# A decoder layer on one core: where four buffers, queues and small calculations are placed

## The chip, the core and the metric

The kernel runs on one core of a Trainium2 chip. The metric is the device time of one execution in microseconds (us). The kernel before was timed three times: 1932.65, 1937.01 and 1935.72 us, median 1935.72 us. A profile of a further execution shows what every engine did: PE (TensorE matmuls), PEld (its weight loads), DVE (VectorE), ACT (ScalarE), POOL (GpSimd) and SP (SyncE, which here only issues DMAs). An engine works through its own list of instructions in order; a DMA issued from SP, ACT or POOL stands in that engine's list as well.

## The reference

One layer over S = 2048 tokens of D = 1024 channels, all in float32. Names are those of the weights.

```python
hn = rms_norm(h, mix_pre_g)
proj = hn @ w_in                            # q, k, v and the GLU input
attn_out = sliding_window_attention(q, k, v, attn_sinks, rel_bias)   # window 128
conv_out = conformer_conv(u, ...)           # GLU, causal conv of 31 taps, LayerNorm, swish, w_conv_pw
mixed = concatenate([attn_out, conv_out]) @ w_out
h = h + rms_norm(mixed, mix_post_g)
hn = rms_norm(h, ffn_pre_g)
ff = (silu(hn @ w_gate) * (hn @ w_up)) @ w_down
h = h + rms_norm(ff, ffn_post_g)
```

## The kernel before, in words

**Precision.** A float32 product is made of three matmuls: each operand is split into a high part (an ACT copy, L888, L782 or L133) and a low part (a DVE subtraction, written through L85), and high x high, high x low and low x high are added up in a PSUM bank. A step of twelve matmuls so needs one ACT copy and one DVE subtraction for its weight tile w@F. There are four PSUM banks named mm, three named tr and one named ct; a bank that PE wants again has to be read out by ACT or DVE first.

**Stages.** Tokens go in four tiles of 512 (w = 0 to 3). A is the input projection, B the attention, C the convolution: its taps are 480 DVE instructions (fc@C<-glu@C), whose results are written to y_scr (L618), loaded again (L630) and turned by PE through the ct bank (L602). W is the output projection of a tile with its norm and residual (`stage_w`, `norm_w`). F is the gate and up projection and G the down projection, both as seven products of half-size blocks (Strassen and Winograd) for two tiles together: first for tiles 0 and 1, then for 2 and 3. `stage_pre` does the first two products of some blocks ahead of time and stores one result of each in the DRAM tensor keeps (from ACT, 36 stores); `stage_p1` does the rest and puts the products of gate and up into the DRAM tensor mids (L1129, L1160, L1166, L1169); `stage_p2` (G) loads these and multiplies with w_down and its block sums.

**Order.** The program is written as one main chain (A, then W of tile 1, F, G, F, G) and lanes beside it (taps, attention, W of tile 0, W of tiles 2 and 3, block sums of w_down) which are advanced by credits as the main chain goes on. A scheduler then sets the final order of the instructions on each engine from these. A buffer name such as fa, chl or gb is a ring with a fixed count of slots: a new user of a slot waits until the last user has been read.

**W of tile 0** runs beside A of tile 2 and 3. `stage_w` loads two rows of mixT at a time (`load`, L804, from SP), ACT and DVE split them (`operand`, L782), PE multiplies (mm@W), ACT copies the first results out of the bank (mid@W, L757). Its first two rows use two slots of the ring fa, which stages A, F and G use as well.

**The norms of W.** `norm_w` needs two reciprocal roots of 128x4 numbers for a tile, each by three Newton steps in `rsqrt`. For w < 3 they are done on POOL (four instructions a step, L159 to L162), for w = 3 on DVE (three a step). ACT then scales the rows by the second one (L873).

**Kept results.** In `stage_p1`, `fetch` (L1097 to L1101) loads the kept result of the next block into a slot of gb, a DMA issued by SP. ACT copies it into a PSUM bank (L1132) before the block's products add to it. There are 19 such loads in F of tiles 0 and 1 and 15 in F of tiles 2 and 3; two further ones are taken from `stage_pre`.

**G's loads.** In `stage_p2` the DRAM rows of mids are loaded one by one (L1237): the first two into the ring at, the others into fa, which still holds the last results of F on their way to mids. The w_down halves go into mb (L1241).

Of the kernel before, what the change touches and what calls it, by code (L numbers as in the profile page):

```python
# [23 lines left out]
D = 1024  # L24
DFF = 2816
P = 128
T = 512
# [10 lines left out]
def layer_kernel(ctx, tc, x, xT, cols, rows, sinks, relb, onehot, w_in, w_four, w_pw, w_out, w_gate, w_up, w_down, out):  # L38
    nc = tc.nc
# [9 lines left out]
    def nm(s):  # L49
        uid[0] += 1  # L50
        return f"{s}@{lab[0]}_{uid[0]}"
# [3 lines left out]
    def t_(tag, shape, dt=F32):  # L55
        return sb.tile(list(shape), dt, tag=tag, name=nm(tag), bufs=BUFS[tag])

    def f4(tag, shape=(P, D)):
        return t_(tag, shape)

    def f2(tag, shape=(P, T)):
        return t_(tag, shape)

    def hl(tag):
        return t_(tag, (P, 2, T), F32R)

    def sm(n, dt=F32):
        kind = "A" if lab[0][0] == "G" else lab[0][0]
        return sb.tile([P, 8], dt, tag="sm" + kind, name=nm("sm"), bufs={"C": 8, "W": 4}.get(kind, 16))[:, 0:n]
# [80 lines left out]
    def rsqrt(ssq, n, mean_over, beside_taps=True):  # L150
        v = sm(n)
        y = sm(n)
        t = sm(n)
        vts(v, ssq, 1.0 / mean_over, EPS, ALU.mult, ALU.add)
        vts(y.bitcast(I32), v.bitcast(I32), 1, None, ALU.logical_shift_right)
        vts(y.bitcast(I32), y.bitcast(I32), -1, 0x5F3759DF, ALU.mult, ALU.add)
        for _ in range(3):
            if beside_taps:
                ptt(t, y, y, ALU.mult)  # L159
                ptt(t, t, v, ALU.mult)  # L160
                nc.gpsimd.tensor_scalar(t, t, -0.5, 1.5, ALU.mult, ALU.add)
                ptt(y, t, y, ALU.mult)  # L162
            else:
                vtt(t, y, y, ALU.mult)
                stt(t, v, -0.5, t, ALU.mult, ALU.mult)
                stt(y, t, 1.5, y, ALU.add, ALU.mult)
        return y
# [453 lines left out]
    def stage_tail(t, sink=None):  # L621
        L = f"C{t}"
        lab[0] = L
        yt = t_("yt", (P, 4, 4 * P))
        ycs = []
        turn = turner(yt, ycs)
        for c in range(4):
            lab[0] = L
            y = f2("fc")
            nc.sync.dma_start(y, y_scr[c, :, t * T : (t + 1) * T])  # L630
            ycs.append(y)
            turn(c)
            yield 0.5
        yield from conv_tail(t, yt, sink)
# [34 lines left out]
    def spare_tile():  # L669
        if not spare:  # L670
            spare.append(t_("mb", (P, 2, T)))
        return spare[0]
# [89 lines left out]
    def load_gb(row):  # L762
        gb = []
        for n in range(2):
            t = f2("gb")
            nc.sync.dma_start(t, rows[row, n * T : (n + 1) * T].partition_broadcast(P))
            gb.append(t)
        return gb

    def post_scale(acc, gb, r):  # L770
        for n in range(2):
            cs = slice(n * T, (n + 1) * T)
            tied(stt(acc[:, cs], acc[:, cs], r, gb[n], ALU.mult, ALU.mult))

    def stage_w(w, spill, G, atag, htag, mtag, bank_of, norm=None):
        L = f"W{w}"
        lab[0] = L
        acc = [f4(atag) for _ in range(4)]

        def operand(m):  # L780
            a = hl(htag)
            act(a[:, 0], m, AF.Copy)  # L782
            vtt(a[:, 1], m, a[:, 0].bitcast(F32), ALU.subtract)
            return [a]

        def acts(gi, ms=None):
            return [operand(m) for m in ms or load(gi)]

        conv = []
        tail = stage_tail(w, lambda v: conv.append(operand(v))) if w > 1 else ()  # L790
        for y in tail:
            if y == YL2:
                break
            yield y
        lab[0] = L

        stage = spare_tile() if w == 1 else None

        def load(gi):
            ms = []  # L800
            pair_ = stage if w == 1 else t_("wx", (P, 2, T)) if w > 1 and gi == 0 else None
            for c in range(G * gi, G * gi + G):
                ms.append(pair_[:, c % 2] if pair_ is not None else f2(mtag))
                nc.sync.dma_start(ms[-1], mixT[c, :, w * T : (w + 1) * T])  # L804
            return ms

        first = load(0)
        gb = load_gb(0) if w > 1 else None
        if w != 1:
            yield 5.0 if w == 0 else 8.0  # L810
            lab[0] = L
        nxt = acts(0, first)
        for gi in range(KC // G):
            if w > 1 and G * gi == 4:
                yield from tail
                lab[0] = L
            aa = nxt if w < 2 or G * gi < 4 else conv[G * gi - 4 : G * gi - 4 + G]
            for n in range(2):
                lab[0] = L
                more = gi + 1 < KC // G and (w < 2 or G * gi + G < 4)  # L820
                if n == 0 and more:
                    if w < 2 and G * gi + G == 4:
                        ld.until(f"C{w}")
                        lab[0] = L
                    rows_next = load(gi + 1)
                if n == 1 and more:
                    nxt = acts(gi + 1, rows_next)
                src = w_out[2 * gi : 2 * gi + 2] if gi < 2 else w_join[2 * gi - 4 : 2 * gi - 2]
                ws = weight(src[:, :, n * T : (n + 1) * T].rearrange("c p t -> p c t"),
                            lo_out[n, 2 * gi : 2 * gi + 2], w > 0, on_pool=False)  # L830
                yield from block_half(acc, list(zip(aa, ws)), n, gi == 0, L, bank_of)
        last = norm_w(w, spill, acc, mtag, gb)
        if norm:
            norm(last)
        else:
            yield from last

    def norm_w(w, spill, acc, mtag, gb):
        L = f"W{w}"
        lab[0] = L  # L840
        gb = gb or load_gb(0)
        ssq = sm(4)
        for s in range(4):
            act(junk, acc[s], AF.Square, accum_out=ssq[:, s : s + 1])
            yield 0.5
            lab[0] = L
        r = rsqrt(ssq, 4, D, w < 3)
        yield 3
        lab[0] = L
        ssq2 = sm(4)  # L850
        for s in range(4):
            lab[0] = L
            post_scale(acc[s], gb, r[:, s : s + 1])
            r0 = w * T + s * P
            if s == (2 if mtag == "fa" else 0):
                xt = f4("wx")
                nc.sync.dma_start(xt, x[r0 : r0 + P])
                vtt(acc[s], xt, acc[s], ALU.add)
            else:
                for n in range(2):  # L860
                    cs = slice(n * T, (n + 1) * T)
                    xt = f2(mtag if s == 1 or w > 1 else "fa")
                    nc.sync.dma_start(xt, x[r0 : r0 + P, cs])
                    vtt(acc[s][:, cs], xt, acc[s][:, cs], ALU.add)
            nc.sync.dma_start(h_scr[r0 : r0 + P], acc[s])
            act(junk, acc[s], AF.Square, accum_out=ssq2[:, s : s + 1])
            yield 5.0
        lab[0] = L
        r2 = rsqrt(ssq2, 4, D, w < 3)
        yield 3  # L870
        lab[0] = L
        for s in range(4):
            act(acc[s], acc[s], AF.Copy, scale=r2[:, s : s + 1])  # L873
            if spill:
                r0 = w * T + s * P
                nc.scalar.dma_start(hn_scr[r0 : r0 + P], acc[s])
        yield 0.1
        hns[w] = acc
# [176 lines left out]
    def stage_p1(ws, ops, mid, keep):  # L1055
# [32 lines left out]
        kept = {}  # L1088
# [8 lines left out]
        def fetch(m):  # L1097
            if m < PRE:
                lab[0] = L
                kept[m] = f2("gb")  # L1100
                nc.sync.dma_start(kept[m], keep[m])  # L1101

        loads(0)
        sums(0)
# [5 lines left out]
        for q, (m, j, i, nst) in enumerate(todo):  # L1110
# [4 lines left out]
            pr = MATS[m][1]  # L1115
# [56 lines left out]
            if j == 1:  # L1172
                fetch(m + 1)
# [44 lines left out]
    def stage_p2(ws, am, td, last=False):  # L1218
# [5 lines left out]
        rawa, rawb, opsd = {}, {}, {}  # L1224
# [7 lines left out]
        def load(i):  # L1232
            if i < len(steps):
                lab[0] = L
                ty, pr = steps[i]
                rawa[i] = f2("fc" if last else "at" if i < 2 else "fa")
                nc.sync.dma_start(rawa[i], am[ty, pr])  # L1237
                if pr % 2 == 0:
                    rb = t_("raw" if last else "mb", (P, 2, T))
                    for j in range(min(2, npr - pr)):  # L1240
                        nc.sync.dma_start(rb[:, j], source(ty, pr + j))  # L1241
                        rawb[i + j] = rb[:, j]
# [16 lines left out]
        kept = {}  # L1259
# [71 lines left out]
        for i in range(nn):  # L1331
            ty, pr = steps[i]
# [20 lines left out]
        for b in range(4):  # L1353
# [3 lines left out]
            ssq = sm(1)  # L1357
# [5 lines left out]
            r = rsqrt_one(ssq, sse[:, b : b + 1])  # L1363
# [248 lines left out]
```

## Time and profile before

| | us |
|---|---|
| median of three runs | 1935.72 |
| the profiled execution | 1937.05 |
| its span, first to last instruction | 1934.7 |
| PE busy in it | 1897.4 |
| DVE busy | 1492.1 |
| ACT busy | 970.4 |
| POOL busy | 211.5 |

The span is 2.35 us shorter than the profiled execution's own time, and the sum of the prediction is made against that own time. PE is busy for 98% of the span, so all that can be gained without leaving work out lies in PE's gaps and in stretches in which its granted clock is below 1. A row of a timeline gives the start, the duration, the engine, the line, what is written and read, how many like instructions follow each other, and in brackets how long the engine stood idle just before and what released it.

### The profile page before, as it was taken

The page shows a single profiled execution, that of the slowest core. Times are in us where ns is not written, and L with a number is a line of the kernel's source. Part 1 is how long each engine was busy: PE and PEld are TensorE (multiplying, and loading weights), DVE is VectorE, ACT ScalarE, POOL GpSimd, SP SyncE. Part 2 cuts the span into 40 slices and gives each one's busy share as a digit, 9 for nine tenths or more (in the row PEclk, how much of TensorE's full clock was granted, in tenths as well). Part 3 has the DMA queues.
Part 4 walks back from the last instruction along what each step waited for, and adds up shares of the span by engine and source line. Part 5 has one row for each costly group of instructions (what it writes and reads, how often), then busy time and mean ns, then how long its engine had stood idle before and what let it go on. Part 6 is the DMA issues. An engine that isn't in the chain of part 4 may idle for free.

```text
span 1934.7 us, 26719 instructions
## 1 busy us (share of the span) xinstructions
PE 1897.4 (98%) x8714; PEld 1535.7 (79%) x8714; DVE 1492.1 (77%) x2760; ACT 970.4 (50%) x1911; POOL 211.5 (11%) x311
## 2 busy tenths in 40 slices
PE   9999998999999999999999999999999999999997
PEld 7777776777778878877878878888888888888886
DVE  6999999887876999988988775788566665455557
ACT  5455444656667433433445574676434333345443
POOL 2010012112010000000000010010033333211000
PEclk9999999999999999999999999999999999999999
DMA  9887756669668775787396687699544443376664
GB/s 332 313 279 234 226 171 213 196 229 342 197 239 283 242 249 200 230 279 266 125 320 224 216 308 233 219 346 314 196 166 151 165 151 109 131 240 193 209 193 156
DMA packets 227707, 439.35 MB, mean 227 GB/s; under 512 B 22728, under 2 KB 48752, under 8 KB 227568
## 3 DMA queue, kind: packets, MB, share of 16 engines
q1 hardware_dynamic: 206256, 403.04, 62.6%
q10 hardware_dynamic: 19392, 28.32, 4.1%
q0 software_dynamic: 1920, 6.29, 0.8%
q8 instruction: 68, 1.11, 0.2%
q14 instruction: 71, 0.58, 0.1%
HBM read 318.54 MB, written 119.02 MB: 226 GB/s over the span
## 4 chain that ended last, share of the span: by engine, by line
PE 67%; DVE 16%; DMA 11%; issue 3%; ACT 1%; POOL 1%; SPq 0%; DVEq 0%; ACTq 0%; POOLq 0%
PE mm@F L108 35%; PE mm@G L108 18%; DVE fc@C L85 7%; PE tr@W L108 4%; PE mm@A L108 4%; PE mm@W L108 3%; PE tr@B L108 1%; DMA glu@C<-glu_scr 1%; DVE w@F L85 1%; DMA mids<-fa@F 1%; DMA chl@F<-w_gate 1%; DVE fa@F L85 1%; DVE p@B L493 1%; DMA wx@G<-w_down 1%; DMA fa@G<-mids 1%
## 5 line engine op out<-in xcount | busy, mean ns | idle before, releaser
L85 DVE SCALAR_TENSOR_TENSOR fc@C<-glu@C,colt,fc@C 128x512 f32<-128x512 f32 x480 | 353.3, 753 | 1.9
L108 PE MATMUL mm@F<-hl@H,w@F 128*128 128x512 f32 x1056 | 254.6, 390 | 0.1
L108 PEld LDWEIGHTS mm@F<-hl@H,w@F 128*128 128x128 f32 x1056 | 197.8, 188 | 42.0 <-ACT gb@F L1143 0.9
L108 PE MATMUL mm@G<-hl@G,hl@G 128*128 128x512 f32 x924 | 226.8, 395 | 3.7 <-ACT hl@G L888 3.0
L108 PEld LDWEIGHTS mm@G<-hl@G,hl@G 128*128 128x128 f32 x924 | 171.5, 189 | 41.6 <-ACT hl@G L888 3.8
L888 ACT ACTIVATE w@F<-chl@F 128x512 fp32r<-128x512 f32 x220 | 135.3, 625 | 130.1 <-PE mm@F L108 124.7
L108 PE MATMUL mm@G<-w@G,hl@G 128*128 128x512 f32 x876 | 199.5, 389 | 0.0
L108 PE MATMUL mm@A<-hl@A,w@A 128*128 128x512 f32 x792 | 192.1, 393 | 1.4 <-DVE w@A L85 1.1
L108 PEld LDWEIGHTS mm@G<-w@G,hl@G 128*128 128x128 f32 x876 | 164.4, 188 | 34.1
L108 PEld LDWEIGHTS mm@A<-hl@A,w@A 128*128 128x128 f32 x792 | 147.0, 188 | 34.6 <-issue 1.7
L85 DVE TENSOR_TENSOR w@F<-chl@F,w@F 128x512 fp32r<-128x512 f32 x198 | 144.2, 732 | 35.3 <-ACT w@F L888 34.9
L108 PE MATMUL mm@F<-mid@H,w@F 128*128 128x512 f32 x528 | 131.3, 392 | 3.5 <-DVE fa@F L85 3.5
L108 PE MATMUL mm@F<-ql@H,w@F 128*128 128x512 f32 x528 | 130.5, 391 | 4.3 <-ACT w@F L888 3.3
L108 PE MATMUL mm@F<-p@H,w@F 128*128 128x512 f32 x528 | 129.0, 389 | 0.0
L108 PE MATMUL mm@F<-x@H,w@F 128*128 128x512 f32 x528 | 128.3, 391 | 0.0
L108 PEld LDWEIGHTS mm@F<-mid@H,w@F 128*128 128x128 f32 x528 | 99.4, 189 | 25.1 <-DVE fa@F L85 4.4
L108 PEld LDWEIGHTS mm@F<-ql@H,w@F 128*128 128x128 f32 x528 | 98.4, 188 | 25.7 <-ACT w@F L888 4.1
L108 PEld LDWEIGHTS mm@F<-x@H,w@F 128*128 128x128 f32 x528 | 98.5, 188 | 21.9 <-ACT w@F L888 0.8
L108 PEld LDWEIGHTS mm@F<-p@H,w@F 128*128 128x128 f32 x528 | 99.0, 188 | 20.7 <-ACT at@F L1146 0.2
L108 PE MATMUL mm@W<-w@W,hl@W 128*128 128x512 f32 x384 | 102.0, 411 | 8.2 <-ACT hl@W L782 5.1
L85 DVE TENSOR_TENSOR w@G<-raw@G,w@G 128x512 fp32r<-128x512 f32 x73 | 51.3, 703 | 67.0 <-ACT w@G L888 66.0
L133 ACT ACTIVATE w@A<-raw@A 128x512 fp32r<-128x512 f32 x104 | 63.0, 624 | 64.6 <-DMA raw@A<-w_in 36.5
(314 smaller groups left out, 3197.7 us busy)
## 6 DMA issues: line engine op xcount, KB each, us to landing
mids<-fa@F SPq DMA_DIRECT2D x154, 256.0 KB, 2.8
raw@A<-w_in SPq DMA_DIRECT2D x52, 512.0 KB, 5.3
w@A<-lo_in SPq DMA_DIRECT2D x84, 256.0 KB, 4.7
fc@G<-mids SPq DMA_DIRECT2D x77, 256.0 KB, 3.5
fa@G<-mids SPq DMA_DIRECT2D x75, 256.0 KB, 4.6
w@W<-lo_out SPq DMA_DIRECT2D x48, 256.0 KB, 3.8
chl@F<-w_gate SPq DMA_DIRECT2D x22, 512.0 KB, 4.0
raw@F<-w_gate SPq DMA_DIRECT2D x22, 512.0 KB, 3.8
```

Of the source, the lines that this page charges most:

```text
L85: r = op(*args, **kw)
L108: r = nc.tensor.matmul(*args, **kw)
L133: act(w[:, 0], raw, AF.Copy)
L493: read = nc.vector.tensor_tensor_reduce(out=pr[:, h], in0=os[g][:, j, P:], in1=bias[0][:, h], op0=ALU.add, op1=ALU.max, scale=1.0, scalar=NEG,
L888: act(w[:, 0], x, AF.Copy)
```

## The change

Four edits, each independent of the others:

```diff
@@ stage_w, load (1) @@
-            pair_ = stage if w == 1 else t_("wx", (P, 2, T)) if w > 1 and gi == 0 else None
+            pair_ = stage if w == 1 else t_("wx", (P, 2, T)) if gi == 0 else None
@@ norm_w (2) @@
-        r = rsqrt(ssq, 4, D, w < 3)
+        r = rsqrt(ssq, 4, D, w == 2)
...
-        r2 = rsqrt(ssq2, 4, D, w < 3)
+        r2 = rsqrt(ssq2, 4, D, w == 2)
@@ stage_p1, fetch (3) @@
-                nc.sync.dma_start(kept[m], keep[m])
+                nc.scalar.dma_start(kept[m], keep[m])
@@ stage_p2, load (4) @@
-                rawa[i] = f2("fc" if last else "at" if i < 2 else "fa")
-                nc.sync.dma_start(rawa[i], am[ty, pr])
+                if not last and i < 8:
+                    if i % 2 == 0:
+                        pair_ = t_("chl", (P, 2, T))
+                        nc.sync.dma_start(pair_, am[ty, pr : pr + 2].rearrange("j p t -> p j t"))
+                        rawa[i], rawa[i + 1] = pair_[:, 0], pair_[:, 1]
+                else:
+                    rawa[i] = f2("fc" if last else "fa")
+                    nc.sync.dma_start(rawa[i], am[ty, pr])
```

(1) The first two rows of W of tile 0 go into the single buffer wx in place of two slots of fa. (2) The roots of tiles 0 and 1 are made on DVE (9 instructions of Newton steps a call) in place of POOL (12 a call); four calls change. (3) The 34 loads of kept results are issued by ACT in place of SP. (4) In the first G the first eight rows of mids come as four loads of two rows each into the ring chl; at is no longer used there, and fa only from the ninth row on.

The scheduler places the instructions anew. Three places show it.

**First place: W of tile 0 beside A.** SP's list before, where the taps' result y_scr, the loads of rows fa@W<-mixT and weights follow each other:

```order
L132 DMA w@A_573_3525<-lo_in 128x512
L143 DMA raw@A_609_3700<-w_in 128x1024
L618 DMA y_scr<-fc@C_420_2645 128x512
L593 DMA glu@C_544_3397<-glu_scr 128x542
L804 DMA fa@W_561_3488<-mixT 128x512
L804 DMA fa@W_562_3490<-mixT 128x512
L383 DMA glu_scr<-fa@A_550_3441 128x512
L804 DMA fa@W_565_3498<-mixT 128x512
L143 DMA raw@W_626_3809<-w_out 128x2x512
L804 DMA fa@W_566_3500<-mixT 128x512
```

And SP's list now (buffer numbers are one lower behind the pair that left the ring):

```order
L132 DMA w@A_572_3524<-lo_in 128x512
L143 DMA raw@A_608_3699<-w_in 128x1024
L804 DMA fa@W_564_3497<-mixT 128x512
L804 DMA fa@W_565_3499<-mixT 128x512
L618 DMA y_scr<-fc@C_420_2645 128x512
L593 DMA glu@C_544_3397<-glu_scr 128x542
L383 DMA glu_scr<-fa@A_550_3441 128x512
```

The loads of the third and fourth row, which stood behind y_scr, stand ahead of it; those of the first two are gone from here and stand some fifty entries earlier, in the wx buffer. On PE the transposes of the taps' result (L602) moved against the projection A. PE's list before:

```order
L602 MATMUL ct@C_593_3637<-ident,fc@C_592_3635 128x128 x4
L108 MATMUL mm@W_656_3959<-w@W_655_3955,hl@W_585_3605 128x512
L535 MATMUL tr@B_672_4051<-ident,p@B_541_3375 128x128 x4
L108 MATMUL mm@A_669_4021<-mid@A_503_3142,w@A_667_4015 128x512 x3
L108 MATMUL mm@A_669_4021<-mid@A_504_3146,w@A_667_4015 128x512 x3
L108 MATMUL mm@A_669_4021<-mid@A_505_3150,w@A_667_4015 128x512 x3
L108 MATMUL mm@A_669_4021<-mid@A_506_3154,w@A_667_4015 128x512 x3
```

PE's list now:

```order
L108 MATMUL mm@A_668_4020<-hl@A_521_3264,w@A_667_4017 128x512 x3
L108 MATMUL mm@A_668_4020<-hl@A_522_3268,w@A_667_4017 128x512 x3
L108 MATMUL mm@A_668_4020<-hl@A_523_3272,w@A_667_4017 128x512 x3
L108 MATMUL mm@A_668_4020<-hl@A_524_3276,w@A_667_4017 128x512 x3
L535 MATMUL tr@B_671_4050<-ident,p@B_541_3375 128x128 x4
L602 MATMUL ct@C_592_3636<-ident,fc@C_591_3634 128x128 x4
```

The 24 matmuls of this block of A, which followed the transposes, now precede them; counted from the program's start, 1772 matmuls stood ahead of them before and 1801 stand there now.

**Second place: the end of W of tile 0 on ACT.** ACT's list before, from the first scaling by the root (L873) to the first copy out of a bank of tile 1 (mid@W, L757):

```order
L873 ACTIVATE x@W_557_3484<-x@W_557_3484,sm@W_777_4666 128x1024
L873 ACTIVATE x@W_558_3485<-x@W_558_3485,sm@W_777_4666 128x1024
L873 ACTIVATE x@W_559_3486<-x@W_559_3486,sm@W_777_4666 128x1024
L782 ACTIVATE hl@W_850_5101<-mb@J_341_2174 128x512
L873 ACTIVATE x@W_560_3487<-x@W_560_3487,sm@W_777_4666 128x1024
L876 DMA hn_scr<-x@W_557_3484 128x1024
L782 ACTIVATE hl@W_851_5104<-mb@J_341_2174 128x512
L876 DMA hn_scr<-x@W_558_3485 128x1024
L445 ACTIVATE ql@A_789_4769<-mm@A_787_4737 128x512
L133 ACTIVATE w@W_838_5030<-raw@W_837_5028 128x512
L133 ACTIVATE w@W_839_5033<-raw@W_837_5028 128x512
L876 DMA hn_scr<-x@W_559_3486 128x1024
```

ACT's list now:

```order
L782 ACTIVATE hl@W_849_5094<-mb@J_341_2174 128x512
L782 ACTIVATE hl@W_850_5097<-mb@J_341_2174 128x512
L445 ACTIVATE ql@A_788_4762<-mm@A_786_4730 128x512
L133 ACTIVATE w@W_837_5023<-raw@W_836_5021 128x512
L133 ACTIVATE w@W_838_5026<-raw@W_836_5021 128x512
L757 ACTIVATE mid@W_789_4775<-mm@W_798_4797 128x512
L873 ACTIVATE x@W_557_3484<-x@W_557_3484,sm@W_776_4662 128x1024
L873 ACTIVATE x@W_558_3485<-x@W_558_3485,sm@W_776_4662 128x1024
L873 ACTIVATE x@W_559_3486<-x@W_559_3486,sm@W_776_4662 128x1024
L873 ACTIVATE x@W_560_3487<-x@W_560_3487,sm@W_776_4662 128x1024
L876 DMA hn_scr<-x@W_557_3484 128x1024
L757 ACTIVATE mid@W_790_4776<-mm@W_813_4887 128x512
```

The splits of tile 1, a copy of A and the first copy out of a bank moved from behind the scalings to ahead of them; the second copy out of a bank still stands behind.

**Third place: kept results in F of tiles 0 and 1.** SP's list before, at the load of the seventeenth (names with 14xx are its block's):

```order
L1193 DMA td<-fc@G_1449_8566 128x512
L1071 DMA chl@F_1471_8744<-w_gate 128x1024
L1193 DMA td<-fc@G_1448_8565 128x512
L1160 DMA mids_4775<-fa@F_1430_8466 128x512
L1101 DMA gb@F_1463_8679<-keeps_4780 128x512
L1166 DMA mids_4775<-fa@F_1430_8466 128x512
```

ACT's list now, at the same load:

```order
L1143 ACTIVATE gb@F_1457_8640<-mm@F_1456_8627 128x512
L1101 DMA gb@F_1462_8666<-keeps_4773 128x512
L888 ACTIVATE w@F_1463_8671<-chl@F_1460_8660 128x512
L1146 ACTIVATE at@F_1459_8658<-mm@F_1455_8625 128x512
L888 ACTIVATE w@F_1465_8691<-chl@F_1460_8660 128x512
L1132 ACTIVATE mm@F_1473_8740<-gb@F_1462_8666 128x512
L888 ACTIVATE w@F_1467_8712<-chl@F_1461_8663 128x512
```

And ACT's list now at the fifteenth load:

```order
L1143 ACTIVATE gb@F_1422_8408<-mm@F_1421_8395 128x512
L888 ACTIVATE w@F_1428_8437<-chl@F_1425_8428 128x512
L1101 DMA gb@F_1427_8434<-keeps_4773 128x512
L1132 ACTIVATE mm@F_1438_8506<-gb@F_1427_8434 128x512
L888 ACTIVATE w@F_1430_8457<-chl@F_1425_8428 128x512
```

The load no longer stands behind stores to td and mids on SP; on ACT it stands ahead of the copy that needs it (L1132), with three instructions between at the seventeenth and none at the fifteenth.

## Prediction

> **What bounds the kernel now.** I read the page first, then the list of what PE waited for, then the timeline around each wait, and last the clock behind it.
>
> ```profile
> PE 1897.4 (98%) x8714; PEld 1535.7 (79%) x8714; DVE 1492.1 (77%) x2760; ACT 970.4 (50%) x1911; POOL 211.5 (11%) x311
> ```
> ```profile
> PE mm@W L108 <- ACT hl@W L782: 5.1, 1, 5.1
> PE mm@F L108 <- DVE fa@F L85: 3.5, 2, 2.7
> ...
> ```
>
> PE is the bound, and the first rows of its waits (total, times, longest) name single waits, not a steady one. A wait costs more than its length if the clock falls. The next rows show the stretches right behind four of them (length, PE busy, PEld, DVE, ACT, POOL, granted clock, DMA share, GB/s).
>
> ```profile
> 327.40:332.40 5.00, 5.00 (x15) 4.06 (x16) 4.26 (x17) 1.22 (x2) 0.43 (x1) 0.67 0.96 279
> 474.70:482.70 8.00, 8.00 (x30) 6.14 (x30) 2.85 (x11) 3.86 (x7) 0.00 (x0) 0.61 0.91 311
> 862.70:867.70 5.00, 5.00 (x15) 3.95 (x16) 5.00 (x9) 2.30 (x4) 0.00 (x0) 0.66 0.79 255
> 999.00:1004.00 5.00, 4.97 (x15) 3.94 (x16) 5.00 (x9) 2.05 (x4) 0.00 (x0) 0.66 1.03 344
> ```
>
> PE was busy there, yet at part of its clock: 5 x 0.33 = 1.65 us, 8 x 0.39 = 3.12, 5 x 0.34 = 1.70 and again 1.70 us of full-speed work are lost. Behind the other waits no such stretch follows. What is gained before 1350 us should arrive at the end, since from there to the end at 1934.7 it is busy all but 10 us, none of them touched by the change:
>
> ```profile
> 1350.00:1935.00 585.00, 574.82 (x2536) 475.62 (x2535) 354.23 (x552) 246.69 (x449) 107.68 (x76) 0.99 0.51 172
> ```
>
> **Part 1, first rows of W.**
>
> ```profile
> 321.99 0.32 SPq L618 DMA_DIRECT2D y_scr<-fc@C  x1
> 322.83 0.93 SPq L804 DMA_DIRECT2D fa@W<-mixT  x2
> ...
> 326.72 1.27 ACT L782 ACTIVATE hl@W<-fa@W 128x512 fp32r<-128x512 f32 x2 [3.91 <-DMA fa@W<-mixT]
> ...
> 327.40 0.80 PE L108 MATMUL mm@W<-w@W,hl@W 128*128 128x512 f32 x1 [5.08 <-ACT hl@W L782]
> ```
> ```profile
> 380.27 0.63 PE L602 MATMUL ct@C<-ident,fc@C 128*128 128x128 f32 x4 [2.49 <-DMA fc@C<-y_scr]
> ```
>
> SP stood at the store of the taps' result; the first rows queued behind it, landed some 4 us later, were split by ACT, and PE stood 5.08 us. In the new order the first two rows are loaded long before, so this wait should go with its clock: 5.08 + 1.65 = 6.73 us. What is late next is the taps' result at 380.27. If it comes as much sooner as the rest, its 2.49 us go as well: 9.2 us is the upper end. If it stays, PE must still stand at 380.27, but with 24 more matmuls of A done by then (first place of the order). Twelve of them took 2.89 us:
>
> ```profile
> 366.20 2.89 PE L108 MATMUL mm@A<-hl@A,w@A 128*128 128x512 f32 x12
> ```
>
> So that is about 5.8 us. The lower end is nought: DVE, which must subtract for the early rows, has no room there (stretch 300 to 330):
>
> ```profile
> 300.00:330.00 30.00, 24.61 (x126) 18.59 (x125) 29.96 (x63) 11.77 (x21) 6.21 (x6) 0.90 0.74 226
> ```
>
> It is busy 29.96 of 30 us, so each subtraction put ahead of a tap delays taps. From 330 to 382 it has room again, 6.9 of 52 us (330 to 350 and 350 to 382 together):
>
> ```profile
> sum 52.00, PE 49.15 PEld 38.00 DVE 45.12 ACT 31.48 POOL 10.09; mean PE 24.57 PEld 19.00 DVE 22.56 ACT 15.74 POOL 5.05
> ```
>
> So I take a value near the second figure, **5.5 us**. The first two loads now stand some fifty entries earlier in SP's list, where SP may wait for the attention rows that they read to reach DRAM; A's weights queue behind. PE then works on weights loaded before; if that cover is too short, it costs up to the 3.9 us that such a row took to land.
>
> **Part 2, roots on DVE.**
>
> ```profile
> 467.10 0.20 POOL L162 TENSOR_TENSOR sm@W<-sm@W,sm@W 128x4 f32<-128x4 f32 x1
> ```
> ```profile
> 467.33 2.19 ACT L873 ACTIVATE x@W<-x@W,sm@W 128x1024 f32<-128x1024 f32 x2 [5.43 <-POOL sm@W L162]
> ...
> 474.07 1.55 ACT L757 ACTIVATE mid@W<-mm@W 128x512 f32<-128x512 f32 x3
> ...
> 474.70 0.79 PE L108 MATMUL mm@W<-w@W,hl@W 128*128 128x512 f32 x1 [2.81 <-ACT mid@W L757]
> ```
>
> POOL's twelve small operations end at 467.30; ACT stood 5.43 us for them, then worked through the scalings, and the copy that frees PE's bank came at 474.07. In the new order that copy stands ahead of the scalings, so PE's 2.81 us and the 3.12 us of clock behind them can go: 5.9 us is the upper end. Price: 9 operations a call on DVE, whose like takes 0.16 us:
>
> ```profile
> 458.67 0.16 DVE L85 TENSOR_SCALAR sm@W<-sm@W 128x4 f32<-128x4 f32 x1
> ...
> 450.00:480.00 30.00, 27.19 (x118) 21.48 (x117) 22.29 (x45) 18.00 (x30) 5.84 (x12) 0.90 1.00 355
> ```
>
> That is 9 x 0.16 = 1.4 us a call, 5.8 for four, and DVE is idle for 7.7 of these 30 us, which covers it; without cover it would be 1.4 us here. The second copy (mid@W) still stands behind four scalings of 1.1 us each. If its bank is needed at once, PE waits 4 x 1.1 less the 12 x 0.24 of one bank's matmuls, 1.5 us, and the clock may fall behind that again: of the 5.9 saved, 1.5 + 3.1 = 4.6 come back, and a gain of 1.3 is the lower end. I take most of the upper end, **4.5 us**.
>
> **Part 3, kept results on ACT's queue.** ACT's and PE's rows of the places that cost time, with SP's issue:
>
> ```profile
> 684.73 0.49 SPq L1101 DMA_DIRECT2D gb@F<-keeps  x1
> ...
> 886.22 0.47 SPq L1101 DMA_DIRECT2D gb@F<-keeps  x1
> ```
> ```profile
> 682.04 0.62 ACT L888 ACTIVATE w@F<-chl@F 128x512 fp32r<-128x512 f32 x1
> 689.59 0.60 ACT L1132 ACTIVATE mm@F<-gb@F 128x512 f32<-128x512 f32 x1 [6.92 <-DMA gb@F<-keeps]
> ...
> 881.04 0.60 ACT L1143 ACTIVATE gb@F<-mm@F 128x512 f32<-128x512 f32 x1 [2.08 <-PE mm@F L108]
> ...
> 890.02 0.60 ACT L1132 ACTIVATE mm@F<-gb@F 128x512 f32<-128x512 f32 x1 [7.86 <-DMA gb@F<-keeps]
> ```
> ```profile
> 690.79 0.73 PE L108 MATMUL mm@F<-ql@H,w@F 128*128 128x512 f32 x2 [1.18 <-ACT w@F L888]
> ...
> 831.00 1.66 PE L108 MATMUL mm@F<-mid@H,w@F 128*128 128x512 f32 x6 [0.86 <-DVE fa@F L85]
> 845.85 1.89 PE L108 MATMUL mm@F<-ql@H,w@F 128*128 128x512 f32 x7 [0.96 <-ACT mm@F L1132]
> 862.69 2.57 PE L108 MATMUL mm@F<-mid@H,w@F 128*128 128x512 f32 x6 [2.67 <-DVE fa@F L85]
> 891.23 0.73 PE L108 MATMUL mm@F<-ql@H,w@F 128*128 128x512 f32 x2 [2.12 <-ACT w@F L888]
> ```
>
> At 690.79 the load could leave ACT at 682.66 instead of 684.73, and at 891.23 at 881.64 instead of 886.22: 2.1 and 4.6 us sooner, enough for gaps of 1.18 and 2.12. I count 831.00 (0.86) with them: 4.2 us. At 845.85 PE waits for the copy itself, which nothing brings forward. At 862.69 PE waits for DVE, which stood for a store to mids and not for a kept load; I leave it, with its 1.70 of clock. Upper end with all five and the clock: 9.5 us. Against it stands that ACT, once it has issued a load, may stand at its copy L1132 until the load lands, with the splits w@F behind it, for which PE waits; at the fifteenth load nothing is in between. From SP's issue to the copy it took 4.9 us at the one place and 3.8 at the other. ACT also takes over 34 issues of about 0.5 us (SP's rows), 17 us on an engine that is idle for half of the span. The groups of twelve matmuls on PE between 837 and 965 are exchanged too. I set 2.7 us against the 4.2 (a gap of 1.0 and one clock stretch of 1.7) and take **1.5 us**; the lower end is the slower rival's loss of 21.9. The Trainium skill's page "DMA: Bandwidth & Descriptors", section "Issuing engines are not separate DMA queues", says that DMAs from SP and ACT run on the same engines and that issuing from several saves only the time of the issue. By that the 3.8 to 4.9 us stay and the part is worth nothing (a rival below); the rows above differ in that SP issued late.
>
> **Part 4, first G.**
>
> ```profile
> 992.46 2.96 SPq L1237 DMA_DIRECT2D fa@G<-mids  x2
> ...
> 998.35 0.63 ACT L888 ACTIVATE hl@G<-fa@G 128x512 fp32r<-128x512 f32 x1 [4.17 <-DMA fa@G<-mids]
> ...
> 999.03 3.25 PE L108 MATMUL mm@G<-hl@G,hl@G 128*128 128x512 f32 x8 [2.41 <-ACT hl@G L888]
> ```
>
> The rows of mids waited for slots of fa that F's last results held; in chl they can be loaded before F's end. The gap and its clock, 2.41 + 1.70 = 4.1 us, are the upper end. Against it, four more splits of G (two rows and two weights) now stand on DVE ahead of F's last results. A like subtraction takes 0.73 us (732 ns in this group):
>
> ```profile
> L85 DVE TENSOR_TENSOR w@F<-chl@F,w@F 128x512 fp32r<-128x512 f32 x198 | 144.2, 732 | 35.3 <-ACT w@F L888 34.9
> ```
>
> That is 2.9 us in which PE's banks stay full: a loss of 2.9 is the lower end. I take **3.0 us**.
>
> **Sum.** 5.5 + 4.5 + 1.5 + 3.0 = 14.5 us. From the profiled execution's 1937.05 us that gives 1922.55. The median of the runs lies 1.33 us below that execution, so 1921.2: I predict **1921 us**.
>
> The Trainium skill's page "TensorE: Matmul & The Clock Gate", "Part 1: The HAM clock gate", has the clock halved only after an idle window of some 3.4 us. By it the stretches behind 474.70 and 999.03 would not hang on gaps of 2.81 and 2.41 us, and would stay. The rows disagree: the clock is 0.61 and 0.66 right behind these gaps.
>
> **The rivals** (all less 1.33 like the forecast).
> - *Every wait goes at its upper end*: 9.2 + 5.9 + 9.5 + 4.1 = 28.7, 1907 us. Against it: at 862.69 PE waits for DVE, on which nothing is taken away there. 5%.
> - *The other queue brings the load no sooner* (the change doesn't do what it says): 14.5 - 1.5 = 13.0, 1923 us. 13%.
> - *The clock stretches come whatever the gaps do*: taken from parts 2 and 4, 2.4 and 1.2 of what I count, so 10.9 us, 1925 us. For it: they may come at fixed times. 5%.
> - *DVE is the bound*: 29.96 of 30 us at 300, and in F
>
> ```profile
> 650.00:820.00 170.00, 168.82 (x743) 139.03 (x742) 160.47 (x260) 66.89 (x120) 0.00 (x0) 1.00 0.70 231
> ```
>
>   it is busy for 160.5 of 170. Then only part 2's 4.5 us are left, 1931 us, half of the cases within 0.2%. Against it: from 330 to 382 DVE has 6.9 idle us, by which its taps can move forward with PE. 18%.
> - *Slower: ACT stands at its own loads.* Five stands of 4.2 to 7.9 us at L1132 went with PE gaps of 0.86 to 2.67, mean 1.56. If all 19 loads of F of tiles 0 and 1 make ACT stand over about 4.2 us, 19 x 1.56 less the 7.8 that five cost already is 21.9 us lost, against 13.0 from the other parts: +8.9, 1945 us. It decides from a stand of some 4 us. In F of tiles 2 and 3 stands up to 5.1 us left no gap, so I count none there:
>
> ```profile
> ACT mm@F L1132 <- DMA gb@F<-keeps: 25.7, 10, 5.1
> ```
>
>   24%.
>
> **How the numbers follow.** The forecast has the remaining 35%. About 0.2% (3.9 us) is what a measurement of this kernel tells from no change. Faster: 35 + 5 + 13 + 5 + half of 18 = 67%; within 0.2%: 9%; slower: 24%. The range runs from 1911, which leaves out the upper-end case, to 1940, which takes in the DVE case and some of the slower one, where fewer loads than 19 make ACT stand.
>
> **What would show it.** Right: no PE wait over 1 us between 320 and 400 and around 470 to 480, a clock near 1 there, and ct@C without a wait; ACT's waits at L1132 in F of tiles 0 and 1 below their total now:
>
> ```profile
> ACT mm@F L1132 <- DMA gb@F<-keeps: 64.7, 18, 7.9
> ```
>
> and no PE wait for hl@G at the start of G. Wrong: new PE waits for w@F behind L1132, PE waiting for x@W or mid@W around 470, DVE at 10 tenths with PE waiting for it after 820, or the gap at 380 as long as the old one at 327.

## The result, and the profile after

The changed kernel takes 1930.69 us (median of 13 runs, 1925.45 to 1934.29) against 1937.68 us (13 runs, 1932.65 to 1944.71). The ratio is 0.9957, 95% interval 0.9944 to 0.9970, that is 8.3 us less by the ratio and 7.0 by the medians. The prediction was 14.5 us. The profiled execution took 1931.2 us, 5.85 less than the one before; its page begins:

```profile
PE 1894.1 (98%) x8714; PEld 1531.8 (79%) x8714; DVE 1497.4 (78%) x2796; ACT 968.5 (50%) x1911; POOL 199.5 (10%) x263
```

The 36 operations more on DVE and 48 fewer on POOL are there (2796 and 263). What PE waited for (total, times, longest) has changed its names:

```profile
PE mm@F L108 <- ACT w@F L888: 4.5, 3, 1.9
PE ct@C L602 <- DMA fc@C<-y_scr: 3.1, 2, 2.1
PE mm@F L108 <- DVE gb@F L85: 2.5, 2, 1.5
...
PE tr@B L535 <- DVE sm@B L493: 1.7, 2, 1.5
...
PE tr@W L108 <- ACT mid@W L757: 1.6, 1, 1.6
PE mm@W L108 <- DVE hl@W L85: 1.6, 1, 1.6
```

The 5.1 us for hl@W and the 3.0 for hl@G are gone from the top. The wait for the taps' result stays (2.9 us in two waits before, 3.1 now), that for the splits w@F in F has grown (3.3 in two before, 4.5 in three), and waits of 1.5 to 1.6 us have come in: for gb@F and hl@W on DVE, for sm@B, for mid@W late in G.

Where it came from can be read by setting the start of the n-th of PE's 8714 matmuls against the start of the n-th in the trace before. At matmul 1457 (300.0 us before) the changed kernel is 1.65 us late, at 2212 (460 us) 0.96 ahead, at 2705 (560) 3.11, at 4436 (960) only 1.32, at 4819 (1050) 6.47, at 5494 (1200) 4.33, at the last 4.56. So parts 1 and 2 brought 4.8 us from the 300 us mark on, F of tiles 0 and 1 lost 1.8, part 4 brought 5.1, and G lost 2.1 again. Below, each run's gain between such marks is given in the same way. It is a reading of single executions: between 300 and 560 us, where their PE lists equal the list of before, e3 gained 1.4 us on it, and e4 and e8 lost 3.0 and 1.7, so a difference of 2 or 3 us there carries no weight by itself. In e1, in e5 and in the kernel before beside e5 to e8 one execution each took far longer (2359, 5433 and 2361 us): the medians below count it, the ratios leave it out, and since the profile of e1 is of that execution, e1 has no reading by marks.

### The profile page after: what moved, and what is told of

Same layout as the page of the kernel before. It is cut to its first block, busy times and chain, and to the rows that moved or that the text cites. A ratio compares the mean times of both kernels' runs of the same rounds, so it can differ in the third digit from the quotient of the medians.

```text
span 1929.5 us, 26650 instructions
## 1 busy us (share of the span) xinstructions
PE 1894.1 (98%) x8714; PEld 1531.8 (79%) x8714; DVE 1497.4 (78%) x2796; ACT 968.5 (50%) x1911; POOL 199.5 (10%) x263
## 4 chain that ended last, share of the span: by engine, by line
PE 65%; DVE 19%; DMA 10%; issue 3%; ACT 1%; POOL 1%; SPq 0%; DVEq 0%; ACTq 0%; POOLq 0%
PE mm@F L108 32%; PE mm@G L108 19%; DVE fc@C L85 8%; PE mm@A L108 4%; PE tr@W L108 4%; PE mm@W L108 2%; DMA glu@C<-glu_scr 1%; DVE w@F L85 1%; DMA mids<-fa@F 1%; DMA wx@G<-w_down 1%; DMA chl@F<-w_gate 1%; DVE chl@F L85 1%; DVE fa@F L85 1%; DMA mixT<-fc@C 1%; PE tr@B L108 1%
```

## The experiments

### Each part alone: e1 to e4

Each kernel is the kernel before with one of the four edits.

> Part 1 alone (first rows of W of tile 0 in wx). Theory A (the taps' result is late next): the 5.1 us wait at 327 goes, but PE waits again for the taps' result (fc@C<-y_scr) near 383, since DVE ends the taps less than 1 us sooner; PE's lead over the kernel before at the same matmul is then 0 to 2.5 us at 460 and in the end, so 1935 to 1938 beside 1937.7. Rival B (as predicted): a lead of 4 us or more at 460 that stays to the end, 1932 to 1934.

> Part 2 alone (roots of tiles 0 and 1 on DVE). Theory A: the wait of 2.8 us at 474 and the slow clock behind it go, a lead of 5 to 6 us at 480, of which about 2 are lost again by 560 because PE then waits for hl@W or hl@H from DVE and ACT near 517; lead in the end 3 to 4 us, 1933 to 1935. Rival B: the lead of 5 us stays, 1932 to 1933.

> Part 3 alone (kept results loaded by ACT). Theory A (in the changed kernel PE lost 1.8 us between 560 and 960): no gain in F of tiles 0 and 1, lead at 960 between -3 and 0, ACT's waits at L1132 there still over 50 us in total; 1937 to 1941. Rival B (as predicted): lead +1 to +4 at 960, 1934 to 1936.5.

> Part 4 alone (first G's rows in pairs in chl). Theory A: lead of 4 to 5 us at 1050 as in the changed kernel, of which about 2.4 are lost near 1153 where PE waits for mid@W; in the end 2 to 3 us, 1934.5 to 1936. Rival B: the loss near 1153 belongs to another part, and 4 to 5 us stay, 1932.5 to 1934.

| run | edit | median us | ratio to before | 95% interval |
|---|---|---|---|---|
| e1 | part 1 | 1929.48 | 0.9962 | 0.9948 to 0.9976 |
| e2 | part 2 | 1932.67 | 0.9980 | 0.9967 to 0.9994 |
| e3 | part 3 | 1936.91 | 1.0005 | 0.9987 to 1.0022 |
| e4 | part 4 | 1932.31 | 0.9972 | 0.9960 to 0.9984 |

Times 1937.4 us, the median of before in these runs, these are gains of 7.4, 3.9 and 5.4 us and a loss of 1.0: 15.7 us in sum, where all four together give 8.3. Theory A's time for part 1 (1935 to 1938) is refuted, and the 1932 to 1934 of its rival are passed too: alone it gives more than was predicted of it. For part 4 the rival is right: the loss near 1153 us is not its own (its lead stays at 2.9 us from 1130 to 1160). Part 2 gains 7.0 us between 460 and 480 and loses 1.5 of them again by 560; its time is that of rival B. Part 3 alone is neither the predicted gain nor clearly a loss; ACT's wait at L1132 in F of tiles 0 and 1 is 56.8 us. The parts do not add, and the question is which pairs don't.

### Pairs and the four without one: e5 to e8

> Parts 1 and 2. Alone they gave 0.9962 and 0.9980. Theory A (they serve the same stretch: what part 1 gains until 380 already takes what part 2 gains at 474, or moves it): no better than part 1 alone, ratio 0.995 to 0.997. Rival B (they add and part 3 is what spoils the sum): 0.9935 to 0.9950.

> Parts 1 and 4, which lie 600 us apart. Alone 0.9962 and 0.9972. If they add: 0.9925 to 0.9945, and the profile shows PE's lead of part 1 at 560 (up to 7 us) kept until 960 and grown by 3 to 5 at 1050. Rival (DVE, busy for over nine tenths from 650 to 1000, takes back what comes earlier): the lead shrinks between 650 and 960 by 2 us or more, ratio 0.995 to 0.997.

> Parts 1, 2 and 4, without the kept results' queue. Theory A (1 and 2 overlap): 0.992 to 0.9945, that is 2 to 6 us faster than the changed kernel's 0.9957 if part 3 costs something beside the others, as its profile's loss of 1.8 us between 560 and 960 says. Rival (part 3 costs nothing, all of the shortfall is overlap): 0.995 to 0.9965.

> Parts 3 and 4. Alone 1.0005 and 0.9972. If they add: 0.997 to 0.998. If part 3's new order of F changes what part 4 meets at the end of F and in G (the changed kernel lost 2.4 us near 1153, the kernel with part 4 alone did not): 0.9985 to 1.0005, with the loss in its profile near 1153.

| run | parts | median us | ratio | 95% interval | if they added |
|---|---|---|---|---|---|
| e5 | 1, 2 | 1929.13 | 0.9958 | 0.9942 to 0.9974 | 0.9942 |
| e6 | 1, 4 | 1922.03 | 0.9925 | 0.9904 to 0.9946 | 0.9934 |
| e7 | 1, 2, 4 | 1924.13 | 0.9929 | 0.9906 to 0.9952 | 0.9914 |
| e8 | 3, 4 | 1937.36 | 0.9999 | 0.9983 to 1.0014 | 0.9977 |
| all | 1, 2, 3, 4 | 1930.69 | 0.9957 | 0.9944 to 0.9970 | 0.9919 |

Parts 1 and 4 add. Part 2 on top of part 1 brings nothing that the interval can tell (0.9962 to 0.9958; with part 4, 0.9925 to 0.9929). Part 3 costs beside others: 0.9929 to 0.9957 on top of parts 1, 2 and 4, 0.9972 to 0.9999 on top of part 4, some 5 us each time. Theory A of e7 stands, and so does the second half of e8's expectation. **Parts 1 and 4 alone, 1922 us, beat both the kernel before and the changed one.**

Why part 2 brings nothing beside part 1 is in e6, which has part 1 and not part 2. ACT's wait for POOL's root and PE's wait behind it:

```profile
466.54 2.19 ACT L873 ACTIVATE x@W<-x@W,sm@W 128x1024 f32<-128x1024 f32 x2 [3.07 <-POOL sm@W L162]
```
```profile
471.55 4.41 PE L108 MATMUL mm@W<-w@W,hl@W 128*128 128x512 f32 x18 [1.69 <-DVE ql@A L85]
```
```profile
471.50:476.50 5.00, 4.95 (x28) 3.91 (x30) 3.75 (x12) 4.80 (x9) 0.00 (x0) 1.00 1.02 392
```

ACT still stands for POOL, for 3.07 us in place of 5.43. PE's wait is 1.69 in place of 2.81, and the clock stays at 1.00 behind it where it was 0.61. e10 (below), with the same PE list there, has 1.69 and 1.00 again, while e3, e4 and e8, which have neither part, wait 3.34, 4.33 and 3.13 us there with a clock of 0.50 to 0.70 in the 5 us behind. Part 1 has taken the 3.1 us of clock that the prediction had put to part 2. With part 2 there (the changed kernel), ACT copies the bank out ahead of the scalings, as the order said, and no wait over 0.7 us is left at 470 to 480:

```profile
470.68 0.58 ACT L757 ACTIVATE mid@W<-mm@W 128x512 f32<-128x512 f32 x1
471.25 1.15 ACT L873 ACTIVATE x@W<-x@W,sm@W 128x1024 f32<-128x1024 f32 x1
```

But some 40 us later PE meets a wait that e6 lacks, for a subtraction that DVE does behind H's work:

```profile
517.64 0.73 PE L108 MATMUL mm@W<-w@W,hl@W 128*128 128x512 f32 x2 [1.59 <-DVE hl@W L85]
```

From matmul 2285 (480 us before) to 2705 the kernels with parts 1 and 2 lose 2.8 to 4.0 us (e5, e7 and the changed one), e6 gains 0.3.

### Is it ACT's stand for its own load? e9 and e10

e9 is the changed kernel, e10 parts 1 and 4, each with the fetch one step earlier:

```diff
                 if pre:
                     bk["B"] = mm()
                     act(bk["B"], kept.pop(m), AF.Copy)
+                fetch(m + 1)
+                lab[0] = L
...
-            if j == 1:
-                fetch(m + 1)
```

> All four parts, with each kept result's load issued one step earlier (ahead of the block's first product instead of behind its second). Three to seven instructions of ACT then stand between a load and its copy L1132 instead of none to five. Theory A (part 3 costs because ACT stands at L1132 for a load that it has just issued, with the splits w@F behind): ACT's waits at L1132 in F of tiles 0 and 1 fall from 56 to under 25 us in total, PE loses nothing between 560 and 960, ratio 0.992 to 0.994, like the kernel without part 3. Rival B (it is the new order of PE's groups and DVE, not ACT's stand): waits at L1132 fall, but PE still loses 1 us or more between 560 and 960, ratio 0.9945 to 0.997.

> Parts 1 and 4 (0.9925 together), kept results' loads on SP as before but issued one step earlier. If ACT's stand at L1132 (56 us in that kernel's F of tiles 0 and 1) is what leaves PE's gaps in F (5.5 us in its profile): a further 2 to 5 us, ratio 0.990 to 0.9915. If those gaps are DVE's: 0.992 to 0.9935.

e9: 1935.12 us, ratio 0.9989 (0.9974 to 1.0003). e10: 1922.47 us, 0.9931 (0.9913 to 0.9949), no different from e6. In the changed kernel ACT's copy L1132 waited for the load almost as long as before (56.5 us in F of tiles 0 and 1 against 64.7). In e9 that wait is gone, and another has its place; the rows are ACT's, then PE's:

```profile
ACT w@F L888 <- PE mm@F L108: 76.0, 35, 4.6
ACT mm@F L1132 <- DVE at@F L85: 49.0, 13, 8.5
```
```profile
PE mm@F L108 <- DVE gb@F L85: 9.2, 7, 3.0
PE mm@F L108 <- DVE fa@F L85: 4.5, 2, 3.9
```

With the load early, the copy waits for the PSUM bank it is to write, which DVE's addition to at@F has to free. PE loses 10.0 us between 560 and 960, and none of its waits there is for splits behind L1132, all are for DVE. So an earlier load does not bring the time of the kernel without part 3, as theory A had it; the ratio misses rival B's range as well. In e10, too, PE waits for no split in F any more (2.4 us in e6), and the time stays.

This does not clear ACT's stand in the changed kernel itself. ACT stands at L1132 in e9 as well (49.0 us), and PE's list in F is not the same in the two. In the changed kernel PE's three waits for w@F, 4.5 us in sum, each come right behind a stand at L1132 (7.06, 7.62 and 3.73 us); e7 and e6 have one each, of 2.34 and 2.39 us. Theory A keeps a share.

### A side way: e11

To shorten the wait for the taps' result near 383 us, e11 takes parts 1 and 4 and lets POOL issue one store that stands ahead of the reload on SP:

```diff
-                nc.sync.dma_start(mixT[4 + c, :, t * T : (t + 1) * T], v)
+                nc.gpsimd.dma_start(mixT[4 + c, :, t * T : (t + 1) * T], v)
```

> Parts 1 and 4, with the store of the convolution's finished rows to mixT (L663) issued by POOL instead of SP, so that the reload of the taps' result no longer stands behind it on SP. Theory A (the wait of 2.2 us at 382 and its slow clock come from that place in SP's list): the reload leaves within 4 us of the taps' result's store instead of 7 to 8, the wait at 382 shrinks below 1 us, a further 2 to 4 us, ratio 0.9905 to 0.992. Rival B (the taps' end on DVE sets it): the wait stays over 1.5 us, 0.992 to 0.9935.

1930.30 us, ratio 0.9968 (0.9954 to 0.9982), slower than e6. The wait at 382 still has 1.4 us, and a new order leaves a worse one at 474.77: PE waits 5.37 us for mid@W, behind scalings for which ACT waited 8.00 us for POOL's root:

```profile
474.77 7.31 PE L108 MATMUL mm@W<-w@W,hl@W 128*128 128x512 f32 x24 [5.37 <-ACT mid@W L757]
```
```profile
467.41 2.19 ACT L873 ACTIVATE x@W<-x@W,sm@W 128x1024 f32<-128x1024 f32 x2 [8.00 <-POOL sm@W L162]
```

SP's rows show the reload not leaving sooner:

```profile
370.25 0.32 SPq L618 DMA_DIRECT2D y_scr<-fc@C  x1
378.63 0.81 SPq L630 DMA_DIRECT2D fc@C<-y_scr  x2
```

It leaves 8.4 us behind the taps' result as in e6 (369.46 and 377.85), without that store ahead of it. What holds it shows among SP's waits in e11, from 365 to 385 us:

```profile
SPq L630 <- DMA mixT<-fc@C: 6.7, 1, 6.7
```

The reload is written into a slot of the ring fc (`stage_tail`), and SP stands at it until a store of finished rows out of that ring to mixT has landed. Whether this store is issued by SP or by POOL, the reload comes behind it.

### The queue or the order that comes with it: e12 to e15

Moving a load to another queue made the scheduler exchange products of F on PE from block 13 on. e12 and e13 tie each product of F of tiles 0 and 1 behind the one before it in the order of the program; e12 is e7 with these ties, e13 the changed kernel. PE's lists are then the same, and DVE's but for four entries.

```diff
-                mat(o, w[:, a, ks], op[k][:, b], start=first and n == 0, stop=n == 11, skip_group_check=not first)
+                r_ = mat(o, w[:, a, ks], op[k][:, b], start=first and n == 0, stop=n == 11, skip_group_check=not first)
+                if row["tie"] and n == 0:
+                    after_first(row["last"], r_)
...
+        row["last"] = r_
...
+            row["tie"] = ws[0] == 0 and 0 < q < 100
```

> Parts 1, 2 and 4 with PE's products in F of tiles 0 and 1 tied to the order of the program (about 100 products, each behind the one before), kept results on SP. It is the base of the next run; its own time tells what the tied order costs beside 0.9929 of the same kernel with a free order. No theory says how much: 0.992 to 0.999.

> The same with part 3 as well: PE's list is now the same instruction for instruction as in the run before, DVE's but for four places; only the queue of the kept results and what follows on ACT and SP differ. Theory C (part 3's cost is the order of PE's products that the scheduler chose for it, in which the product that waits for a bank from DVE comes one product sooner): equal to the run before within 1.5 us, PE loses the same from 560 to 960 in both. Theory A (ACT's stand for its own load): 3 us or more slower than the run before, with waits for w@F.

e12: 1956.22 us, 1.0101 (1.0078 to 1.0123). e13: 1955.25 us, 1.0102 (1.0080 to 1.0123). Equal within 1 us, as theory C says; and an edit of the order of the same products, with all that the scheduler then places anew, costs 32 us against e7. In both PE waits in the same place:

```profile
PE mm@F L108 <- ACT at@F L1153: 27.4, 19, 3.6
```
```profile
PE mm@F L108 <- ACT at@F L1153: 26.8, 19, 2.3
```

Such waits may cover what the queue costs. So e14 and e15 cross queue and order with a single tie each. In e14 (all four parts) the last product of block 12 is put behind the fourth of block 13; PE then has e7's list but for 32 of some 8600 entries. In e15 (e7) it is the other way round, and PE has the changed kernel's list but for 51.

```diff
+    behind = {64: [68]}      # e14
+    behind = {68: [64]}      # e15
...
+                if n == 0:
+                    row[q, 0] = r_
+                    for p_ in behind.get(q, ()):
+                        if (p_, 1) in row:
+                            after_first(row[p_, 1], r_)
...
+        for q2, ps_ in behind.items():
+            if q in ps_ and (q2, 0) in row and q2 < q:
+                after_first(r_, row[q2, 0])
```

> All four parts, kept results on ACT, and one tie: the last product of block 12 of F of tiles 0 and 1 follows the fourth of block 13 on PE. With that the scheduler gives PE the list of the kernel without part 3, but for 32 of 8635 matmuls. Theory C (the order that came with part 3 costs, not the queue): like the kernel without part 3, 0.992 to 0.9945, and PE loses nothing between 560 and 960 nor near 1153. Theory A (the queue costs): like the changed kernel, 0.995 to 0.997.

> The opposite: parts 1, 2 and 4, kept results on SP, with a tie that gives PE the list of the changed kernel but for 51 matmuls (the fourth product of block 13 follows the last of block 12). Theory C: like the changed kernel, 0.995 to 0.997, with losses of PE between 560 and 960 and of 2 us near 1153. Theory A: like the kernel without part 3, 0.992 to 0.9945.

| kept results on, PE's order | run | median us | ratio | 560 to 960 | 1050 to 1200 |
|---|---|---|---|---|---|
| SP, SP's | e7 | 1924.13 | 0.9929 | 3.9 gained | 0.3 lost |
| SP, ACT's | e15 | 1924.87 | 0.9949 (0.9929 to 0.9969) | 0.2 gained | 2.3 lost |
| ACT, SP's | e14 | 1927.87 | 0.9961 (0.9947 to 0.9976) | 1.3 gained | 0.0 |
| ACT, ACT's | changed kernel | 1930.69 | 0.9957 | 1.8 lost | 2.1 lost |

Neither theory has it alone. The loss in G follows the order whatever the queue: 2.1 to 3.8 us in the changed kernel, e8, e9, e10 and e15, which share one PE list between these marks, none over 0.3 in e4, e6, e7, e11 and e14, which share another (e12 and e13, with a third, lose 0.4 and 1.4). In the changed kernel it is this row, which e7 does not have:

```profile
1153.03 2.34 PE L108 MATMUL tr@W<-w@W,ql@W 128*128 128x512 f32 x9 [1.64 <-ACT mid@W L757]
```

In F the order costs about 3.4 us by these profiles (3.7 and 3.1) and the queue about 2.3 (2.6 and 2.0), each near the spread of single executions. The ratios don't confirm it: by them the order costs 3.9 us with SP's queue and nothing (-0.8) with ACT's, the queue 6.2 us in SP's order and 1.5 in ACT's, with intervals of some 4 to 6 us on either side. (The ratios are to the kernel before as it was timed beside each run, some 1937 us with e7 and 1935.01 with e14 and e15, and so they order the rows otherwise than the medians do.) e14 and e15 were timed beside each other, and there the profiles mislead: e14, with ACT's queue, is the slower by 3.0 us in the medians and 2.5 (0.6 to 4.4) in the means, though their profiled executions took 1926.8 and 1927.28 us. So the queue costs more than the order in these two. That part 3 costs beside the others is shown, by e8 against e4 and by the changed kernel against e7, and that both queue and order have a share is likely; how the cost divides is not settled.

One place where the order can be seen at work: PE in the changed kernel, then in e7, at the same block.

```profile
832.00 2.88 PE L108 MATMUL mm@F<-ql@H,w@F 128*128 128x512 f32 x12
835.84 1.65 PE L108 MATMUL mm@F<-yt@H,w@F 128*128 128x512 f32 x6 [0.96 <-DVE gb@F L85]
```
```profile
829.47 2.88 PE L108 MATMUL mm@F<-ql@H,w@F 128*128 128x512 f32 x12
832.19 2.88 PE L108 MATMUL mm@F<-hl@H,w@F 128*128 128x512 f32 x12
834.91 1.52 PE L108 MATMUL mm@F<-yt@H,w@F 128*128 128x512 f32 x6
```

DVE's addition that frees the bank, in the changed kernel and in e7:

```profile
835.11 0.68 DVE L85 TENSOR_TENSOR gb@F<-gb@F,mm@F 128x512 f32<-128x512 f32 x1
```
```profile
832.74 0.68 DVE L85 TENSOR_TENSOR gb@F<-gb@F,mm@F 128x512 f32<-128x512 f32 x1
```

In e7 the addition ends at 833.42 while PE works on the hl@H product, and the yt@H product finds its bank free. In the changed kernel the yt@H product comes one place sooner, and PE stands 0.96 us until the addition ends at 835.79.

## Why the prediction was right in direction and wrong in size

**Part 1, 5.5 us predicted.** Alone it gives 7.4 (4.6 to 10.1). The wait at 327 is gone and its slow clock with it (e6 has a new wait of 2.07 us at 337.75 with a clock of 0.66 behind, the changed kernel one of 0.93 without). What failed is the step behind it. The prediction let the taps' result come sooner or stay at 380.27 with 24 more matmuls done, 5.8 us. It came later, at 383.78, though its store left 0.5 us sooner. SP's rows, before and in the changed kernel, then a wait of SP in the changed kernel (365 to 385 us) and PE's row:

```profile
371.28 0.32 SPq L618 DMA_DIRECT2D y_scr<-fc@C  x1
373.73 0.32 SPq L630 DMA_DIRECT2D fc@C<-y_scr  x1
```
```profile
370.76 0.32 SPq L618 DMA_DIRECT2D y_scr<-fc@C  x1
379.05 0.38 SPq L630 DMA_DIRECT2D fc@C<-y_scr  x1
```
```profile
SPq L663 <- DVE fc@C L85: 6.0, 2, 5.6
```
```profile
383.78 0.48 PE L602 MATMUL ct@C<-ident,fc@C 128*128 128x128 f32 x1 [2.10 <-DMA fc@C<-y_scr]
```
```profile
383.80:388.80 5.00, 5.00 (x18) 4.19 (x19) 4.86 (x12) 4.60 (x20) 0.23 (x1) 0.67 0.92 283
```

The store to y_scr landed after 6.3 us in place of 2.4, and SP then stood at a store to mixT (L663, at 378.64) for DVE before the reload could leave. From the store to PE's row it took 13.0 us in place of 9.0; it was 8.9 to 9.5 in the five kernels traced without part 1 and 11.8 to 13.3 in the eleven with it (e1 aside). So 5.8 less 3.5, 2.3 us, is what was left (2.6 by the marks from 300 to 460), and a further 5 x 0.33 = 1.65 us of clock went behind the wait of 2.10. The kernels with part 1 gained 0.8 to 3.7 us from 300 to 460 (e11, with another list, 5.3). The signs "ct@C without a wait" and "no PE wait over 1 us" between 320 and 400 were wrong; a tr@B wait of 1.50 us at 355.70 came too. In e6 2.0 us were gained up to 460, 4.1 from there to 560, where the full clock at 474 counts, and 2.9 in F, which the prediction gave to no part; why F gains there is open. That the total comes near 5.5 is luck: little of it arose where it was counted.

**Part 2, 4.5 us.** Alone 3.9 (1.2 to 6.4): mechanism and size right. The signs at 470 to 480 are as predicted: no wait over 1 us, clock 1.00. What failed is the sum of it with part 1: 3.1 of the 5.9 us were clock lost behind a wait that part 1 shortens too, and the two terms were added as if each had a gap of its own. On top of part 1, part 2 gives 0.8 us or -0.8, both within the noise.

**Part 3, 1.5 us.** Here the step itself failed, and its sign: alone 1.0 lost (within the interval), beside the others some 5 lost. The step is the 4.2 us that an earlier issue was to save: the loads at 684.73 and 886.22 were to leave 2.1 and 4.6 us sooner, as soon as ACT was free. But a load also needs its slot of gb, and DVE was still reading it. In the kernel before, DVE's reading ends at 684.33 and SP's load leaves 0.40 us later:

```profile
683.65 0.68 DVE L85 TENSOR_TENSOR fa@F<-fa@F,gb@F 128x512 f32<-128x512 f32 x1
```

In the changed kernel, at the same load, ACT's leaves 0.04 us behind it; DVE's row, then ACT's, then PE's:

```profile
680.64 0.68 DVE L85 TENSOR_TENSOR fa@F<-fa@F,gb@F 128x512 f32<-128x512 f32 x1
```
```profile
681.36 0.35 ACTq L1101 DMA_DIRECT2D gb@F<-keeps  x1
686.65 0.60 ACT L1132 ACTIVATE mm@F<-gb@F 128x512 f32<-128x512 f32 x1 [7.06 <-DMA gb@F<-keeps]
```
```profile
687.86 0.73 PE L108 MATMUL mm@F<-ql@H,w@F 128*128 128x512 f32 x2 [1.32 <-ACT w@F L888]
```

So 0.4 us could be saved there and not 2.1, and PE's wait of 1.18 is 1.32 now. At 886.22 it is the same (the reading ends at 885.81); only the load at 824.74, counted with the gap of 0.86, stood some 3 us longer than its slot needed. Of the 19 loads of F of tiles 0 and 1, 13 left within 0.41 us of such a reading by DVE or ACT before, and 13 within 0.04 us do now. The rival "the other queue brings the load no sooner" had this right, apart from the loss that came on top. The wait of 2.12 at 891 is gone (its stand fell from 7.86 to 2.63), but PE now waits 1.88 us for a split behind a stand of 7.62 at 857.05, with a clock of 0.66 behind, and 1.27 behind one of 3.73 at 915.61. That is the sign that the prediction gave for the slower rival, in three places and not at 19 loads: mechanism in part right, size far too large.

The rest is the exchanged groups, which the prediction named in one sentence without a price of their own. Against e7 the changed kernel loses 5.7 us in F by the marks; its waits for w@F are longer by 2.2 us, with one slow stretch of clock behind (1.7 us) that e7 lacks and e6 has, those for gb@F on DVE are longer by 1.9, and those for fa@F shorter by 0.9. In G the order that goes with part 3 costs 2.1 us and more.

**Part 4, 3.0 us.** Alone 5.4 (3.1 to 7.7). By the marks each kernel that has it gains 5.0 to 5.3 us between 960 and 1050 (4.95 in e4, 4.96 in e6, 4.95 in e7); without it e2 gained 2.0 there, and e3 and e5 lost 1.6 and 2.9, with waits of 2.5 to 3.7 us for hl@G. The 5.0 us are the upper end, 4.1, and a little more; the price of 2.9 for four splits on DVE was not paid. From 980 to 1020 PE is busy throughout in the changed kernel:

```profile
980.00:1020.00 40.00, 40.00 (x184) 33.13 (x183) 37.81 (x59) 19.47 (x36) 0.00 (x0) 1.00 0.82 274
```

**The sum.** 5.5 + 4.5 + 1.5 + 3.0 = 14.5 predicted. Taken one upon the other, as the runs allow: part 1 7.4, part 2 on it 0.8, part 4 on both 5.6 (0.9958 to 0.9929), part 3 on all -5.4, which gives the 8.3 us measured, to rounding. Parts 1 and 4, which stand apart in time, were undervalued together by 4.5 us; the two that share a place with another, or that reorder a long stretch, were overvalued by 10.6. The errors cancel in part. The time of the rival "DVE is the bound", 1931 us, is the one measured, but by chance: it leaves the gain to part 2 alone, and parts 1 and 4 without part 2 give more than the whole change.

## What to carry to other kernels

Two waits that one stretch of the trace shows are not two gains: an engine that is freed at the first arrives sooner at the second, whose length and whose slow clock then change. A change of queue or buffer that makes a scheduler exchange groups of work on the bound engine has to be priced by that exchange: look at which bank or buffer each group needs that moves up, and who frees it. The same question goes for the transfer: if its buffer is freed just before it is issued, another queue brings it no sooner. When four small edits go in together, run each alone and leave each out once: here two of the four give 1922 us, and all four 1931.

## What the runs showed of the hardware

The clock does not fall by the length of the wait alone. It was 0.61 behind a wait of 2.81 us at 474 in the kernel before and 0.67 behind 2.10 at 383 in the changed one, but 1.00 behind 1.69 in e6 at the same place, and 1.00 behind 2.12 us at 891 before. In F of the changed kernel it was 0.66 behind 1.88 us at 857, in F of e14 1.00 behind 2.68 us at 885. The Trainium skill, "TensorE: Matmul & The Clock Gate", section "Part 1: The HAM clock gate", tells of a free-running window of some 3.4 us, whose phase differs from run to run; waits of nearly equal length with and without a fall agree with that part, while falls behind waits shorter than 3.4 us do not agree with its idle limit.

The store of the taps' result took 2.4 us to land in the five kernels traced without part 1. It took 5.1 to 6.6 us in the ten in which a load of raw@A left SP some 0.7 us ahead of it, and 3.2 in e11, where the last issue was 3.8 us ahead. That the load ahead slows the store is likely and was not tested by itself.
